# Convolution inputs of a hybrid decoder mixer: transposed by VectorE and transfers in place of TensorE

## The chip, the cores and the metric

The kernel runs on one core of one Trainium2 chip. The metric is the device time of one execution in microseconds; lower is better. Times below are the median of three runs and one profiled execution of the kernel before.

## What is computed

Two layers, each `h += 1/2 norm(SwiGLU(norm(h)))`, then `h += norm(mixer(norm(h)))`, then a second half SwiGLU, on 256 tokens of width 1024 (feed-forward width 2816), all in float32. The mixer projects its input into the columns of three branches; the change concerns the state-space branch (and the feed-forward parts):

```python
q, k, v, z, xbc, dt_raw, u, vg, gate_raw = jnp.split(xn @ w_in, split_at, axis=-1)
xbc = jax.nn.silu(causal_depthwise_conv(xbc, conv_w, conv_b))   # 1536 channels, 4 taps along the tokens
xs, bm, cm = jnp.split(xbc, [SSM_WIDTH, SSM_WIDTH + SSM_GROUPS * SSM_STATE], axis=-1)
dt = jax.nn.softplus(dt_raw.astype(F32) + dt_bias.astype(F32))
y_s = ssd_scan(xs, dt, a, bm, cm) + d_skip[:, None] * xs
```

## The kernel before

**Weights.** All weight matrices are one list of 496 blocks of 128 x 1024 float32. `load` (L160, on SP's queue) brings a block into one of 6 `raw` buffers; `split` makes of it a high part `whi` on ScalarE (L180) and a low part `wlo` on VectorE (L181), in one of 11 pairs of buffers; a matrix product on TensorE takes three matmuls (L213 to L215), high by high, low by high, high by low. Tokens are two tiles of 128.

**The order.** It is written out by the program itself. `gemm` emits the work of TensorE in units of one block and one token tile, six matmuls of 512 columns. After each unit `pump` counts 1.3 us of planned time, steps the tasks that are due (`tick`), and emits the split of one more block if there is one to do. A task is a generator; what it yields is the planned time until its next step, from the table `W`. `finish` steps tasks without regard to what is due, until they have ended. What is emitted first stands first on each engine, and each engine works in that order and waits where data or buffers are not there. A chunk of a projection (512 columns) is eight units.

**Start of a mixer.** `project("xbc", nch=2)` computes the first two chunks of xbc and spawns a task `conv` for each; then come the chunk xbc2 with the third `conv`, z0, z1, the time step (`dt_task`), q0, q1, k and v. In `conv` ScalarE scales the chunk into `xtok` (two tiles, tokens on partitions, L504), TensorE transposes 128 x 128 pieces of it into PSUM (`transposed`, L513), and ScalarE copies them into `xc` (channels on partitions, L516). Then ScalarE writes the last tap and the bias (L535), VectorE adds three taps (L541, twelve instructions a convolution), ScalarE applies silu (L544), and TensorE transposes the result: of convolutions 0 and 1 into `xstr`, which ScalarE copies to `xs` (tokens on partitions again, L553), and the part B of convolution 2 into `btr`. `dt_task` computes `dtps` on TensorE, a chain of small VectorE operations between two exponentials of ScalarE (`dte` L588, `ea` L606), and with the sums `acsT` and `acs` (L620 to L628) what `ssd` starts from. PSUM has five banks for products (`acc`) and three for all else (`tr`). Ahead of `dt_task` the kernel calls `finish(*cv)`, ahead of `ssd` `finish(dte, *ze)`.

**Feed-forward part.** For each of its six chunks `evac` makes `hh`, which `swap_out` transposes in 32 x 32 squares on VectorE into `xt` (L277) and writes to DRAM in one transfer a tile (L279); `swap_in` reads it back in four transfers a tile into `hr` (L286), so that the whole is transposed; then it is split into `hTh` and `hTl` for the down projection (`dn`).

Of the kernel before, what the change touches and what calls it, by code (L numbers as in the profile page):

```python
# [44 lines left out]
ACC, TR = 5, 3  # L45


W = {'gw': 6.5, 'tr': 0, 'parts': 0, 'sq': 1.3, 'lead': 3.9, 'sq2': 5.2, 'hh': 5.2, 'x0': 0.65, 'cv': 5.2, 'cs': 6.5, 'xs': 0, 'dt1': 2.6, 'dt2': 0, 'dt3': 5.2, 'cb': 2.6, 'w1': 1.3, 'w2': 5.2, 'ys': 3.9, 'qk': 3.9, 'vv': 0, 'qs': 0, 'ex': 0, 'p1': 10.4, 'p2': 0, 'p3': 3.9, 'ge': 0, 'ln': 10.4, 'sv': 0, 'yc': 9.1, 'mg': 3.9, 'out': 6.5, 'in': 6.5}


@with_exitstack
def trunk(ctx, tc, a):
# [11 lines left out]
    def b4(name, shape=(P, 1024), dt=F32):  # L64
        return big.tile(list(shape), dt, name=name, tag="b4", bufs=B4)

    def b2(name, shape=(P, 512), dt=F32):
        return big.tile(list(shape), dt, name=name, tag="b2", bufs=B2)
# [203 lines left out]

    def swap_out(src, w):
        xt = b2("xt")
        V.transpose(xt[:, :w], src[:, :w])  # L277
        rd = dram.tile([P, w], F32, name=f"swap{w}", tag=f"swap{w}", bufs=8)
        nc.sync.dma_start(rd, xt[:, :w])  # L279
        return rd  # L280

    def swap_in(dst, rd):

        v = rd.rearrange("(a i) (c e) -> c i a e", a=4, c=4)
        for c in range(4):
            nc.sync.dma_start(dst[32 * c:32 * c + 32], v[c])  # L286

    def halves(ps, hi, lo):

# [105 lines left out]
    def ffn(x, r2, nxt, head=HOLD):  # L395
        hT = {}
        es = {}

        def evac(c, w, gate, up):
            silu, hh = {}, {}  # L400
            for t in range(NT):
                while gate(t) is None:
                    yield 0
                silu[t] = b2("silu")
                A.activation(silu[t][:, :w], gate(t), AF.Silu, scale=r2[t])  # L405
            for t in range(NT):
                while up(t) is None:
                    yield 0
                hh[t] = b2("hh")
                V.scalar_tensor_tensor(hh[t][:, :w], up(t), r2[t], silu[t][:, :w], op0=ALU.mult, op1=ALU.mult)  # L410
            n = w // P
            rd = {t: swap_out(hh[t], w) for t in range(NT)}
            yield W["out"]
            hr = {}
            for t in range(NT):
                hr[t] = b2("hr")
                swap_in(hr[t][:, :w].rearrange("p (a e) -> p a e", a=4), rd[t])
            yield W["in"]
            new = b4 if n > 2 else b2
            hT[c] = (new("hTh", (P, NT, n, P), F32R), new("hTl", (P, NT, n, P), F32R))  # L420
            for t in range(NT):
                hi, lo = (z[:, t].rearrange("p k (a j) -> p a k j", a=4) for z in hT[c])
                r4 = hr[t][:, :w].rearrange("p (a k j) -> p a k j", a=4, k=n)
                A.copy(hi, r4)
                V.tensor_tensor(lo, r4, hi.bitcast(F32), op=ALU.subtract)
                yield 0.65

        def gated(c, w):
            slots, dst = accs("gu")
            full = set()  # L430

            def part(key, o):
                return lambda t: slots[key, t][:, o:o + w] if (key, t) in full else None

            halves_ = 2 if w == 512 else 1
            items = [b for key in range(halves_) for b in chunk(key)]
            es[c] = spawn(evac(c, w, part(0, 0), part(1, 0) if halves_ == 2 else part(0, w)))
            gemm(items, x.h, x.l, dst, head=head if c == 0 else 0, on_done=lambda key, t: full.add((key, t)))

        for c, w in enumerate(FCH):  # L440
            gated(c, w)
        items = [[(k, 512 * j, 512, j, k == 0, k == KF - 1) for j in range(2)] for k in range(KF)]

        def hx(i):
            def get(k, t):
                finish(es[k // 4])
                return hT[k // 4][i][:, t, k % 4, :]
            return get

        slots, dst = accs("dn")  # L450
        after = After(slots, nxt)
        gemm(items, hx(0), hx(1), dst, tail=HOLD, on_done=after, ends=nxt[-1] is not None)
        return after.tasks
# [24 lines left out]
    def mixer(l, x, r2, nxt):  # L478
# [20 lines left out]
        def tokens(ps, scales, name):  # L499

            out = []
            for t in range(NT):
                o = b2(name)
                A.activation(o, ps[t], AF.Copy, scale=scales[t])  # L504
                out.append(o)
            return out
# [18 lines left out]

        def conv(c, ps):
            toks = tokens(ps, r2, "xtok")
            xc = b4("xc", (P, 4, S))
            yield W["x0"]
            yield from transposed(toks, lambda t: xc[:, :, t * P:(t + 1) * P], "a")  # L530
            o = b4("conv", (P, 4, S))
            w = lambda j, k: pl[:, G_CW + 4 * (4 * c + j) + k:G_CW + 4 * (4 * c + j) + k + 1]
            for j in range(4):
                ct = 4 * c + j
                A.activation(o[:, j, :], xc[:, j, :], AF.Identity, scale=w(j, 3),  # L535
                             bias=pl[:, G_CB + ct:G_CB + ct + 1])
            for jj in (0, 2):
                for k in range(3):
                    s = 3 - k
                    for j in (jj, jj + 1):  # L540
                        V.scalar_tensor_tensor(o[:, j, s:], xc[:, j, :S - s], w(j, k), o[:, j, s:],  # L541
                                               op0=ALU.mult, op1=ALU.add)
                yield W["cv"]
            A.activation(o, o, AF.Silu)  # L544
            yield W["cs"]
            if c < 2:
                for t in range(NT):
                    if t not in xs:
                        xs[t] = b4(f"xs{t}")
                    pt = tr("xstr")  # L550
                    for j in range(4):
                        T.transpose(pt[:, j * P:(j + 1) * P], o[:, j, t * P:(t + 1) * P], ident)
                    A.copy(xs[t][:, 512 * c:512 * c + 512], pt)  # L553
                    yield W["xs"]
            else:
                bc["T"] = o
                pt = tr("btr")
                for g in range(SG):
                    T.transpose(pt[:, g * P:(g + 1) * P], o[:, g, 0:P], ident)
                bc["b"] = b2("btok", (P, SG * P))  # L560
                A.copy(bc["b"], pt[:, :SG * P])
# [345 lines left out]
        factors()  # L907
        cv.append(spawn(conv(2, project("xbc")[0])))
        ze = [spawn(z_evac(c, project("z")[0])) for c in range(2)]
        finish(*cv)  # L910
        dte = spawn(dt_task(wdt[l]))
        at = [spawn(qk_evac("q", 0, project("q")[0]))]
        finish(dte, *ze)
        ss = spawn(ssd(ysx, rs))
        at.append(spawn(qk_evac("q", 1, project("q")[0])))
        for c in range(2):
# [218 lines left out]
```

## Time and profile before

| | |
|---|---|
| median of 3 runs | 1486.92 us (1486.62 to 1488.68) |
| profiled execution | 1487.98 us |
| its span, first to last instruction | 1486.2 us |
| TensorE busy | 1472.1 us, 99% |
| VectorE busy | 955.2 us, 64% |
| ScalarE busy | 782.6 us, 53% |
| DMA, share of 16 engines on SP's queue | 60.6%, 291.84 MB |
| chain of waits | TensorE 94%, VectorE 4%, ScalarE 1%, issue 1% |

The span is the time between the first and the last instruction; the execution has 1.78 us more around it. Busy time is the time in which an engine had an instruction at work; of TensorE it contains overlap, since a matmul of 390 ns follows the one before after 227 ns. The chain of waits goes back from the last instruction, at each step to what released it.

### The profile page before, as it was taken

Reading aid. Unit: us, or ns where it says so; the run is one execution under the profiler, and the core shown is the slowest. Engines: PE = TensorE matmul, PEld = TensorE weight load, DVE = VectorE, ACT = ScalarE, POOL = GpSimd, SP = SyncE. Lnnn points to the kernel's source line nnn. Section 1 sums busy time; section 2 is a strip of 40 time slices with the busy share of each in tenths; the row PEclk is TensorE's granted clock in tenths of the full one; section 3 lists DMA queues with packets and bytes.
Section 4 is the critical chain, followed back from the end, with each engine's and each line's share of the span. In section 5 each row is a group of like instructions: output and inputs, shape, how many; then the busy total and the mean of one; then the engine's idle time right before and its main releaser. Section 6 shows DMA issues by size and latency. Waiting matters only on the chain.

```text
span 1486.2 us, 18786 instructions
## 1 busy us (share of the span) xinstructions
PE 1472.1 (99%) x6850; PEld 1218.8 (82%) x6850; DVE 955.2 (64%) x1160; ACT 782.6 (53%) x1079; POOL 55.6 (4%) x98
## 2 busy tenths in 40 slices
PE   9999999999999999999999999999999999999998
PEld 7888888878888888888888888888788888888886
DVE  6766477766666857656486564876665667676652
ACT  6644367555374536544364543765554645464441
POOL 0000020000000000000000000200000000000000
PEclk9999999999999999999999999999999999999999
DMA  8987655335556445888568784654354564478860
GB/s 291 323 253 236 199 190 179 127 115 184 159 181 217 168 154 198 283 230 259 163 230 256 235 253 132 224 167 135 119 192 141 194 204 170 134 272 261 238 200 29
DMA packets 112476, 293.37 MB, mean 197 GB/s; under 512 B 16896, under 2 KB 41600, under 8 KB 112384
## 3 DMA queue, kind: packets, MB, share of 16 engines
q1 hardware_dynamic: 111808, 291.84, 60.6%
q8 instruction: 54, 0.88, 0.2%
q10 hardware_dynamic: 576, 0.33, 0.1%
q14 instruction: 38, 0.31, 0.1%
HBM read 279.54 MB, written 12.58 MB: 197 GB/s over the span
## 4 chain that ended last, share of the span: by engine, by line
PE 94%; DVE 4%; ACT 1%; issue 1%; POOL 0%; DMA 0%; DVEq 0%; ACTq 0%; POOLq 0%
PE gu L213 11%; PE gu L215 11%; PE gu L214 11%; PE dn L213 5%; PE dn L215 5%; PE dn L214 5%; PE br L213 3%; PE br L215 3%; PE br L214 3%; PE gate L215 2%; PE gate L213 2%; PE gate L214 2%; DVE wlo L181 2%; PE xbc L215 1%; PE xbc L213 1%; PE xbc L214 1%
## 5 line engine op out<-in xcount | busy, mean ns | idle before, releaser
L181 DVE TENSOR_TENSOR wlo<-raw,whi 128x1024 fp32r<-128x1024 f32 x495 | 600.2, 1232 | 331.1 <-ACT whi L180 319.8
L180 ACT CAST whi<-raw 128x1024 fp32r<-128x1024 f32 x495 | 512.8, 1051 | 380.9 <-PE gu L215 131.8
L213 PE MATMUL gu<-whi,xh 128*128 128x512 f32 x704 | 276.0, 392 | 1.4 <-ACT xh L316 1.4
L214 PE MATMUL gu<-wlo,xh 128*128 128x512 f32 x704 | 274.9, 391 | 0.0
L215 PE MATMUL gu<-whi,xl 128*128 128x512 f32 x704 | 274.8, 390 | 0.0
L213 PEld LDWEIGHTS gu<-whi,xh 128*128 128x128 f32 x704 | 132.7, 188 | 29.8 <-ACT xh L316 1.8
L215 PEld LDWEIGHTS gu<-whi,xl 128*128 128x128 f32 x704 | 132.6, 188 | 28.0 <-DVE xl L317 0.4
L214 PEld LDWEIGHTS gu<-wlo,xh 128*128 128x128 f32 x704 | 132.5, 188 | 27.9 <-DVE wlo L169 0.9
L213 PE MATMUL dn<-whi,hTh 128*128 128x512 f32 x352 | 137.5, 391 | 0.0
L215 PE MATMUL dn<-whi,hTl 128*128 128x512 f32 x352 | 137.0, 389 | 0.0
L214 PE MATMUL dn<-wlo,hTh 128*128 128x512 f32 x352 | 136.9, 389 | 0.0
L215 PEld LDWEIGHTS dn<-whi,hTl 128*128 128x128 f32 x352 | 66.1, 188 | 13.8
L213 PE MATMUL gate<-whi,xh 128*128 128x512 f32 x192 | 77.3, 403 | 0.0
L214 PEld LDWEIGHTS dn<-wlo,hTh 128*128 128x128 f32 x352 | 66.1, 188 | 13.5
L213 PEld LDWEIGHTS dn<-whi,hTh 128*128 128x128 f32 x352 | 66.1, 188 | 13.4
L215 PE MATMUL gate<-whi,xl 128*128 128x512 f32 x192 | 75.0, 391 | 0.0
L214 PE MATMUL gate<-wlo,xh 128*128 128x512 f32 x192 | 74.8, 390 | 0.0
L316 ACT CAST xh<-xg 128x512 fp32r<-128x512 f32 (+1 forms) x25 | 15.1, 603 | 62.3 <-DVE xg L314 62.3
L215 PEld LDWEIGHTS gate<-whi,xl 128*128 128x128 f32 x192 | 36.0, 188 | 7.7
L405 ACT ACTIVATE silu<-gu,r 128x512 f32<-128x512 f32 (+1 forms) x48 | 31.3, 654 | 19.8 <-PE gu L215 16.2
L214 PEld LDWEIGHTS gate<-wlo,xh 128*128 128x128 f32 x192 | 36.2, 188 | 6.6
L213 PEld LDWEIGHTS gate<-whi,xh 128*128 128x128 f32 x192 | 36.1, 188 | 6.6
(243 smaller groups left out, 2248.3 us busy)
## 6 DMA issues: line engine op xcount, KB each, us to landing
raw<-in_mix SPq DMA_DIRECT2D x232, 512.0 KB, 4.2
raw<-in_gu SPq DMA_DIRECT2D x175, 512.0 KB, 4.9
raw<-in_dn SPq DMA_DIRECT2D x88, 512.0 KB, 4.5
swap<-xt SPq DMA_DIRECT2D x40, 256.0 KB, 3.2
hr<-swap SPq DMA_DIRECT2D x160, 64.0 KB, 4.9
row_ffn_post_g<-in_ffn_post_g SPq DMA_DIRECT2D x4, 512.0 KB, 7.0
swap<-xt SPq DMA_DIRECT2D x8, 128.0 KB, 4.4
hr<-swap SPq DMA_DIRECT2D x32, 32.0 KB, 6.1
```

What stands on the lines that cost most here:

```text
L180: A.copy(hi, w)
L181: V.tensor_tensor(lo, w, hi.bitcast(F32), op=ALU.subtract)
L213: T.matmul(o, xh(k, t), hi[:, off:off + n], start=first, stop=False)
L214: T.matmul(o, xh(k, t), lo[:, off:off + n], start=False, stop=False)
L215: T.matmul(o, xl(k, t), hi[:, off:off + n], start=False, stop=last)
L316: A.copy(o_h, xg)
L405: A.activation(silu[t][:, :w], gate(t), AF.Silu, scale=r2[t])
```

## The change

The feed-forward part transposes `hh` in its own buffer and writes it in four transfers a tile (`turn`), and one transfer a tile reads it back into the same buffer (`land`). The convolution's input no longer goes through TensorE: VectorE transposes `xtok` in place in 32 x 32 squares, four transfers a tile write it to DRAM in pieces of 32 numbers (128 bytes), 512 pieces a transfer (`turn_whole`), and one transfer a convolution reads it into `xc` (`land_whole`). The read can only be issued after the writes have landed. Between the steps stand new yields (2.6, `out`, `in`), and in `W` `out` goes from 6.5 to 7.8 and `in` from 6.5 to 9.1. `finish(*cv)` moves from ahead of `dt_task` to behind q0.

```diff
-W = {... 'out': 6.5, 'in': 6.5}
+W = {... 'out': 7.8, 'in': 9.1}
...
-    def swap_out(src, w):
-        xt = b2("xt")
-        V.transpose(xt[:, :w], src[:, :w])
-        rd = dram.tile([P, w], F32, name=f"swap{w}", tag=f"swap{w}", bufs=8)
-        nc.sync.dma_start(rd, xt[:, :w])
+    def turn(src, m, e=128):
+        V.transpose(src, src)
+        rd = dram.tile([m, 4, 32, 4, e], F32, name=f"turn{m}_{e}", tag=f"turn{m}_{e}", bufs=8)
+        for b in range(4):
+            nc.sync.dma_start(rd[:, :, :, b, :].rearrange("m c i e -> i (m c) e"),
+                              src[32 * b:32 * b + 32].rearrange("p (x e) -> p x e", e=e))
         return rd
...
+    def land(dst, rd):
+        nc.sync.dma_start(dst, rd.rearrange("m c i a e -> (c i) m (a e)"))
+
+    def turn_whole(toks):
+
+        rd = dram.tile([4, P, S], F32, name="turnw", tag="turnw", bufs=6)
+        v = rd.rearrange("k (c i) (t a j) -> t a i (k c) j", c=4, a=4, t=NT)
+        for t in range(NT):
+            V.transpose(toks[t], toks[t])
+            for b in range(4):
+                nc.sync.dma_start(v[t, b], toks[t][32 * b:32 * b + 32, :].rearrange("p (b j) -> p b j", j=32))
+        return rd
+
+    def land_whole(o, rd):
+        nc.sync.dma_start(o, rd.rearrange("k p e -> p k e"))
...
             n = w // P
-            rd = {t: swap_out(hh[t], w) for t in range(NT)}
+            rd = {t: turn(hh[t][:, :w], 1, w // 4) for t in range(NT)}
             yield W["out"]
-            hr = {}
-            for t in range(NT):
-                hr[t] = b2("hr")
-                swap_in(hr[t][:, :w].rearrange("p (a e) -> p a e", a=4), rd[t])
+            for t in range(NT):
+                land(hh[t][:, None, :w], rd[t])
             yield W["in"]
...
         def conv(c, ps):
             toks = tokens(ps, r2, "xtok")
+            yield 2.6
+            rd = turn_whole(toks)
+            yield W["out"]
             xc = b4("xc", (P, 4, S))
-            yield W["x0"]
-            yield from transposed(toks, lambda t: xc[:, :, t * P:(t + 1) * P], "a")
+            land_whole(xc, rd)
+            yield W["in"]
...
         ze = [spawn(z_evac(c, project("z")[0])) for c in range(2)]
-        finish(*cv)
         dte = spawn(dt_task(wdt[l]))
         at = [spawn(qk_evac("q", 0, project("q")[0]))]
-        finish(dte, *ze)
+        finish(dte, *ze, *cv)
```

The changed kernel's lines are twelve higher from L300 on. The transfers of the first mixer's convolutions on SP's queue are new; between weight blocks (`raw`) stand the writes (`turnw`) of convolutions 0 and 1, their reads (`xc`), and the same of convolution 2:

```order
L160 DMA raw<-in_mix 128x1024 x26
L294 DMA turnw<-xtok 32x16x32 x16
L160 DMA raw<-in_mix 128x1024 x3
L298 DMA xc<-turnw 128x4x256 x2
L160 DMA raw<-in_mix 128x1024
L294 DMA turnw<-xtok 32x16x32 x8
L160 DMA raw<-in_mix 128x1024 x3
L298 DMA xc<-turnw 128x4x256
```

Before, only `raw` stands there; now 24 writes and three reads stand between, each read behind the writes it needs.

On TensorE at the end of the chunk q0 of the first mixer, before (the six matmuls of q are the first unit of q1, `cb` the first of `ssd`):

```order
L620 MATMUL acsT<-con,dtg 40x128 x4
L627 MATMUL acs<-dta,con 128x32
L628 MATMUL acs<-dta,ones 128x16
L213 MATMUL q<-whi,xh_1619 128x512
L214 MATMUL q<-wlo,xh_1619 128x512
L215 MATMUL q<-whi,xl_1620 128x512
```

And now:

```order
L633 MATMUL acsT<-con,dtg 40x128 x4
L640 MATMUL acs<-dta,con 128x32
L641 MATMUL acs<-dta,ones 128x16
L565 MATMUL xstr<-con,conv 128x128 x16
L572 MATMUL btr<-con,conv 128x128 x2
L213 MATMUL q<-whi,xh_1595 128x512
```

The eighteen transposes of the convolutions' results, which stood in three places among z0 and z1, stand in one piece between `acs` and q1.

On ScalarE at the same place, from the copy of `dtps` to `dec`, before:

```order
L572 COPY dtT<-dtps 32x256
L180 CAST whi<-raw 128x1024
L588 ACT_TABLE_LOAD
L588 ACTIVATE dte<-dtav 128x32
L606 ACTIVATE ea<-hpar 128x16
L180 CAST whi<-raw 128x1024 x3
L624 CAST acsr<-acsT 40x512
L632 ACTIVATE eac<-acs 128x16
L635 ACTIVATE dec<-dec 128x16
```

And now, from the same copy, and (second piece) from `dec` on:

```order
L585 COPY dtT<-dtps 32x256
L548 ACTIVATE conv<-xc,par 128x256 x4
L180 CAST whi<-raw 128x1024
L601 ACT_TABLE_LOAD
L601 ACTIVATE dte<-dtav 128x32
L557 ACT_TABLE_LOAD
L557 ACTIVATE conv<-conv 128x1024 x2
L619 ACT_TABLE_LOAD
L619 ACTIVATE ea<-hpar 128x16
L180 CAST whi<-raw 128x1024 x3
L637 CAST acsr<-acsT 40x512
L645 ACTIVATE eac<-acs 128x16
```

```order
L648 ACTIVATE dec<-dec 128x16
L566 COPY xs_2376<-xstr 128x512
L566 COPY xs_2383<-xstr 128x512
L566 COPY xs_2376<-xstr 128x512
L566 COPY xs_2383<-xstr 128x512
L557 ACT_TABLE_LOAD
L557 ACTIVATE conv<-conv 128x1024
L574 COPY btok<-btr 128x256
```

The silus (L557) stand between the exponentials and behind `dec`, each with a table load of its own; the copies of `xstr` have moved behind `dec`. On VectorE the same piece now has, between `dtg` and `acsr`, two splits, the last six taps of convolution 2 and a split, where three splits stood; ahead of `dtav` stand the 24 taps of convolutions 0 and 1, the first six of convolution 2 and five splits from the first tap on, in the order 12 taps, three splits, 12 taps, a split, 6 taps, a split.

## Rows read from the trace of the kernel before

**Rows 1.** page, part 1: busy us, share and instructions of each engine

```profile
PE 1472.1 (99%) x6850; PEld 1218.8 (82%) x6850; DVE 955.2 (64%) x1160; ACT 782.6 (53%) x1079; POOL 55.6 (4%) x98
```

**Rows 2.** chain of waits: start us, us, what; transposes of two convolution inputs

```profile
218.52 0.87 PE ctr L513 x8
```

**Rows 3.** timeline of ScalarE, first mixer: start us, us, instruction, [idle before]

```profile
222.22 4.08 ACT L535 ACTIVATE conv<-xc,par 128x256 f32<-128x256 f32 x8
...
237.04 2.00 ACT L544 ACTIVATE conv<-conv 128x1024 f32<-128x1024 f32 x2
...
246.23 1.07 ACT L553 COPY xs<-xstr 128x512 f32<-128x512 f32 x2 [2.10 <-PE xstr L552]
...
259.08 1.28 ACT L588 ACT_TABLE_LOAD   x1
260.94 0.23 ACT L588 ACTIVATE dte<-dtav 128x32 f32<-128x32 f32 x1 [0.58 <-DVE dtav L586]
261.08 0.20 ACT L606 ACTIVATE ea<-hpar 128x16 f32<-128x16 f32 x1
...
270.66 0.22 ACT L635 ACTIVATE dec<-dec 128x16 f32<-128x16 f32 x1 [0.24 <-DVE dec L634]
```

**Rows 4.** timeline of VectorE over the same stretch

```profile
221.44 1.23 DVE L181 TENSOR_TENSOR wlo<-raw,whi 128x1024 fp32r<-128x1024 f32 x1 [0.70 <-ACT whi L180]
222.91 4.91 DVE L541 SCALAR_TENSOR_TENSOR conv<-xc,par,conv 128x253 f32<-128x253 f32 x12 [0.25 <-ACT conv L535]
227.74 3.50 DVE L181 TENSOR_TENSOR wlo<-raw,whi 128x1024 fp32r<-128x1024 f32 x3
231.14 4.82 DVE L541 SCALAR_TENSOR_TENSOR conv<-xc,par,conv 128x253 f32<-128x253 f32 x12
...
260.31 0.37 DVE L582 SCALAR_TENSOR_TENSOR dtv<-dtps,r,hpar 128x16 f32<-128x16 f32 x2
...
264.67 0.20 DVE L609 SCALAR_TENSOR_TENSOR dta<-dt,ea 128x32 f32<-128x32 f32 x1
264.97 0.29 DVE L616 COPY dtg<-dta 128x32 f32<-128x32 f32 x2
...
269.29 0.68 DVE L625 TENSOR_TENSOR acsr<-acsT,acsr 8x512 fp32r<-8x512 f32 x1
```

**Rows 5.** timeline of TensorE, from the end of q0 to q1

```profile
266.85 1.07 PE L620 MATMUL acsT<-con,dtg 128*40 128x128 f32 x8
...
268.32 0.48 PE L213 MATMUL q<-whi,xh 128*128 128x512 f32 x1
```

**Rows 6.** groups by line, VectorE: count | busy us, mean ns | idle before

```profile
L277 DVE STREAM_TRANSPOSE xt<-hh 128x512 f32<-128x512 f32 (+1 forms) x48 | 29.0, 642 | 0.0
```

**Rows 7.** windows (last: clock, DMA share, GB/s); DMA packets from 699.5 to 700.5

```profile
214.00:218.00 4.00, 4.00 (x19) 3.21 (x18) 3.10 (x3) 3.73 (x6) 0.00 (x0) 1.00 1.02 417
...
226.00:230.00 4.00, 4.00 (x19) 3.30 (x18) 4.00 (x7) 3.68 (x5) 0.00 (x0) 1.00 0.05 10
...
DMA packets 338, 0.08 MB, mean 84 GB/s; under 512 B 336, under 2 KB 336, under 8 KB 338
...
q1 hardware_dynamic: 338, 0.08, 37.1%
```

**Rows 8.** transfers of L286, the feed-forward part's reads

```profile
DMA to landing us min/median/max: 1.7/4.9/8.1
```

**Rows 9.** timeline of TensorE and windows after a wait of the first mixer

```profile
310.79 0.63 PE L513 MATMUL ctr<-con,qtok 128*128 128x128 f32 x4 [1.58 <-DVE ssw L682]
...
312.00:314.00 2.00, 2.00 (x6) 1.56 (x5) 1.95 (x3) 1.44 (x3) 0.00 (x0) 0.50 0.00 0
314.00:316.00 2.00, 2.00 (x7) 1.59 (x6) 1.62 (x2) 0.34 (x2) 0.00 (x0) 0.65 0.03 2
```

**Rows 10.** tiles hr and dn, first feed-forward part: ns, first and last start

```profile
L425 DVE TENSOR_TENSOR hTl<-hr,hTh x4: 418/556/686, 137.4 to 151.3; 128x512 fp32r<-128x512 f32 x2, 128x256 fp32r<-128x256 f32 x2
...
L213 PE MATMUL dn<-whi,hTh x88: 389/389/481, 132.2 to 192.2; 128*128 128x512 f32 x88
```

More of the change, by code (lines that the diff above doesn't have):

```diff
@@ L45 @@
 ACC, TR = 5, 3
-W = {'gw': 6.5, 'tr': 0, 'parts': 0, 'sq': 1.3, 'lead': 3.9, 'sq2': 5.2, 'hh': 5.2, 'x0': 0.65, 'cv': 5.2, 'cs': 6.5, 'xs': 0, 'dt1': 2.6, 'dt2': 0, 'dt3': 5.2, 'cb': 2.6, 'w1': 1.3, 'w2': 5.2, 'ys': 3.9, 'qk': 3.9, 'vv': 0, 'qs': 0, 'ex': 0, 'p1': 10.4, 'p2': 0, 'p3': 3.9, 'ge': 0, 'ln': 10.4, 'sv': 0, 'yc': 9.1, 'mg': 3.9, 'out': 6.5, 'in': 6.5}
+W = {'gw': 6.5, 'tr': 0, 'parts': 0, 'sq': 1.3, 'lead': 3.9, 'sq2': 5.2, 'hh': 5.2, 'x0': 0.65, 'cv': 5.2, 'cs': 6.5, 'xs': 0, 'dt1': 2.6, 'dt2': 0, 'dt3': 5.2, 'cb': 2.6, 'w1': 1.3, 'w2': 5.2, 'ys': 3.9, 'qk': 3.9, 'vv': 0, 'qs': 0, 'ex': 0, 'p1': 10.4, 'p2': 0, 'p3': 3.9, 'ge': 0, 'ln': 10.4, 'sv': 0, 'yc': 9.1, 'mg': 3.9, 'out': 7.8, 'in': 9.1}
 @with_exitstack
@@ L271, in sumsq @@
         return ss
-    def swap_out(src, w):
-        xt = b2("xt")
-        V.transpose(xt[:, :w], src[:, :w])
-        rd = dram.tile([P, w], F32, name=f"swap{w}", tag=f"swap{w}", bufs=8)
-        nc.sync.dma_start(rd, xt[:, :w])
-        return rd
[L282 to L286, printed above, removed]
+    def turn(src, m, e=128):
[4 more added lines that the diff above has]
+                              src[32 * b:32 * b + 32].rearrange("p (x e) -> p x e", e=e))
+        return rd
+    def land(dst, rd):
[10 more added lines that the diff above has]
+        nc.sync.dma_start(o, rd.rearrange("k p e -> p k e"))
     def halves(ps, hi, lo):
@@ L422, in evac @@
                 hi, lo = (z[:, t].rearrange("p k (a j) -> p a k j", a=4) for z in hT[c])
-                r4 = hr[t][:, :w].rearrange("p (a k j) -> p a k j", a=4, k=n)
+                r4 = hh[t][:, :w].rearrange("p (a k j) -> p a k j", a=4, k=n)
                 A.copy(hi, r4)
```

## Prediction

> **What bounds the kernel now.** I read the page first: TensorE is busy 1472.1 of 1486.2 us [rows 1], and the chain of waits is 94% TensorE. So an instruction taken off TensorE shortens the kernel by its own time, and an instruction that TensorE has to wait for lengthens it by the wait, at once; ScalarE and VectorE count only where TensorE's next instruction needs their result. Next I read the chain for the transposes that go [rows 2], then the timelines of ScalarE and VectorE over the first mixer's start [rows 3, 4] and the two TensorE rows at the end of its first q chunk [rows 5]. The reader is to see there that in the kernel before the three convolutions are so far by 246.23 that their first outputs are copied [rows 3], long before that point, and that the last step into the q1 chunk, at 268.32, is not waited for. The timeline of the second mixer has the same pieces with the same durations, so I work out one layer and double it.
>
> **What is removed.** Each layer has four groups of input transposes: two of eight instructions at 0.87 us [rows 2] and two of four, at half of it. That is 2.62 us a layer, 5.2 us in all, from the path. ScalarE loses six copies a layer and VectorE gains six in-place transposes of 0.64 us [rows 6]; both lie beside TensorE's work.
>
> **What is added: the trip of the inputs.** The order on VectorE puts the four transposes of convolutions 0 and 1 behind the same split that ended at 222.7 [rows 4]; at 0.64 us each they run to about 225.3, the first write being issued about two transposes in. The DMA engines were full until then (share 1.02 at 214 to 218) and free after 226 (0.05) [rows 7], so the writes flow from about 225. Sixteen transfers of 512 packets of 128 bytes are 8192 packets. No packet of 128 bytes is in the trace. The nearest row is the stretch with 336 packets of 256 bytes: share 37.1% of 16 engines for 1 us over 338 packets, 17.6 ns each [rows 7]. With that price, 8192 x 17.6 / 16 = 9.0 us, done at 234.0. Lower bound half of it (4.5 us, price by bytes), upper bound double (18 us, because these are writes of pieces half as long as any in the row); I take the row itself. Three weight blocks stand between on SP, 0.524 MB each at 417 GB/s [rows 7], 3.8 us, then the read back of the first 0.5 MB, 1.3 us, and at least 1.7 us to land [rows 8]: the first convolution's input is there at **241** (236.5 with the lower bound, 250 with the upper). In the kernel before its first activation began at 222.22 [rows 3]. SP waits for the writes there, with weight loads queued behind it; ten split blocks stand ahead of TensorE, 27 us of its work, so that wait alone starves nobody before about 264.
>
> The Trainium skill, page "DMA: Bandwidth & Descriptors", section "Specifications", says that below 512 bytes a DMA engine does a read-modify-write; no row here shows a write so short. By it I would take the upper bound, 250, and the sum below would be 18 us larger.
>
> **What is moved: the convolutions into the end of q0.** Planned steps are in units of one weight block and one token tile (six matmuls). The yields of a convolution now end beyond the chunk at which it is asked for: the order shows the sixteen output transposes and the two of B forced out in one piece behind acsT, ahead of q1. From the arrival X of the input the engines, which work in order, need:
> - VectorE: first tap 0.7 us behind the first activation; 12 taps 4.9, three weight splits 3.5, 12 taps 4.8, a split 1.2, six taps of convolution 2 at half of twelve, 2.5, a split 1.2, and 0.6 for dtv (0.37) and dtav (0.2, as dta) [rows 4]: X+19.4.
> - ScalarE: dte 0.2, a table load 1.3, the two silus 2.0, a table load back 1.3, ea 0.2 [rows 3]: X+24.4. The loads are new here, because silu now stands between two exponentials; eight more in the program.
> - VectorE: dta and dtg, 0.6 [rows 4]: X+25.0. Only now can acsT start. With the input at 241 that is 266.0; TensorE would be there at 266.85 (its start before [rows 5]) less 2.62 and less the eighteen transposes that used to lie ahead (18 x 0.109 = 2.0, same form as [rows 2]), 262.2. A first wait of 3.8 us.
> - VectorE after it, in order: two splits with a short wait for their other half 2.8, the last six taps 2.5, a split 1.2: X+31.5; then acsr to ScalarE's dec 1.6 [rows 3, 4]: X+33.1. Two of the four transpose groups wait here, since only three PSUM buffers serve them.
> - ScalarE: four xs copies 2.1, a table load 1.3, silu of convolution 2 1.1 [rows 3], then the transposes of B 0.3: **X+37.9**, when q1 can start.
>
> With X = 241 q1 starts at 278.9, against 268.32 before [rows 5]: 10.6 us later a layer, the removed 2.62 us being inside (the wait is 13.2 us). Two layers: 21.2 us. A wait of that length also costs clock: before, after a wait of 1.58 us that ended at 310.79, the granted clock stood at 0.50, the 1.2 GHz level, for the 2 us from 312 and averaged 0.65 over the next 2, some 3.4 us at that level [rows 9], 1.7 us lost. I add 1.7 us a layer, 3.4 (none and 3.4 a layer are the bounds). **Sum: 21.2 + 3.4 = 24.6 us.**
>
> The Trainium skill, page "ScalarE: Activation LUTs", section "What ACT_TABLE_LOAD costs", puts 1.38 us of drain on top of each load; in the trace the load that began at 259.08 and took 1.28 has dte behind it at 260.94, and that waited 0.58 us for VectorE's dtav, for nothing else [rows 3]; I leave the drain out. By the page three loads a layer on the path would add 8.3 us to the sum.
>
> **Feed-forward part: nothing.** It has as many transfers a chunk as before (eight out and two in, for two and eight), as many transposes, and no row of TensorE waits for hT. The new distances put the last chunk 3.9 us later. Its split ended near 152 where the down projection began at 132.2 [rows 10], and that projection has sixteen blocks (16 x 2.7 = 43 us) ahead of the chunk: 20 us of cover. If it were gone, 3.9 us for each of four feed-forward parts.
>
> **The rivals.** (a) The forecast, +24.6 us: 1511.5. (b) The short writes cost double: X = 250, q1 19.6 us later a layer, 39.2 + 3.4 = +42.6 us: 1529.5. For it: nothing in the trace shows that SBUF can be written out in such pieces at the price of longer reads. Against it: the engines are free at that time. (c) On the other side, the trip and the chain are hidden: if X + 37.9 comes ahead of 265.7 (268.32 less 2.62), q1 waits for nothing and the gain is the 5.2 us: 1481.7. That decides at X = 227.8, and breaks even at 230.4. Against it: the transposes alone end at 225.3. For it: parts of my chain might overlap more than the order lets me see. (d) Half hidden, with a wait of some 2.6 us a layer that eats the gain: no change. (e) TensorE runs out of split weights too, because VectorE holds its splits behind taps that wait for data: needs X beyond 257, and gives over 1535.
>
> **How the numbers follow.** The profiled execution took 1487.98 us, 1.78 more than its span; the median of the runs is 1486.92, 1.06 below it. I add the sum to the median: 1486.92 + 24.6 = **1511.5**. Chances: (a) 0.60, (b) 0.22, (c) 0.07, (d) 0.05, (e) 0.06. Range: at the lower bound of the packets X = 236.5, q1 6.1 us later a layer, and no clock lost: +12.2, 1499; I begin the range at 1500. Its upper end is (b) with somewhat more clock lost, 1531. Left out are (c), (d) and (e), 0.18. What a measurement of this kernel can tell from no change is 0.2%, 3 us: faster 0.07, within it 0.05, slower 0.88.
>
> **What would show it.** In the profile after: TensorE idle 11 to 22 us in each mixer between the end of q0 and the start of q1, put down to ScalarE or VectorE at acsT, xstr and btr; a stretch at clock 0.50 there; 14 table loads for 6; the first conv activation some 20 us behind xtok; SP waiting for turnw. Wrong: the first conv activation within 12 us of xtok (then (c)); q1 later than 282 (then (b)); waits of TensorE in the feed-forward parts; or a wait at q0's end without the clock falling.

## The result, and the profile after

The changed kernel takes 1513.68 us, median of 4 runs (1513.32 to 1515.19), beside 1487.63 us for the kernel before on the same chip: ratio 1.0177, 95% interval [1.0165, 1.019]. The forecast was 1511.5, the range 1500 to 1531. The profiled execution took 1513.51 us with a span of 1511.7.

Part 1 of the page after, to be held against [rows 1]:

```profile
PE 1476.1 (98%) x6802; PEld 1221.0 (81%) x6802; DVE 958.4 (63%) x1172; ACT 787.4 (52%) x1075; POOL 57.7 (4%) x98
```

Span less busy time of TensorE was 14.1 us before (1486.2 - 1472.1) and is 35.6 now (1511.7 - 1476.1): 21.5 us more waiting. Busy time rose by 4.0 us although 5.2 us of transposes are gone, because some matmuls run at the lower clock. The view of waits over the whole span, TensorE after (line, released by whom: us in all, times, longest), has three entries that the kernel before does not have:

```profile
PE acsT L633 <- DVE dtg L629: 8.9, 2, 4.8
PE btr L572 <- ACT conv L557: 6.1, 2, 3.0
PE xstr L565 <- DVE acsr L638: 6.1, 2, 3.0
```

21.1 us together, each once in each mixer. There is no new wait in the feed-forward parts. (In `conv` and behind it the lines are thirteen higher, not twelve: L620 before is L633 now.) The timeline of TensorE at the place of [rows 5], first mixer:

```profile
266.43 1.90 PE L633 MATMUL acsT<-con,dtg 128*40 128x128 f32 x8 [4.07 <-DVE dtg L629]
...
273.26 2.82 PE L565 MATMUL xstr<-con,conv 128*128 128x128 f32 x12 [3.04 <-DVE acsr L638]
279.13 0.69 PE L572 MATMUL btr<-con,conv 128*128 128x128 f32 x2 [3.04 <-ACT conv L557]
279.47 0.78 PE L213 MATMUL q<-whi,xh 128*128 128x512 f32 x1
```

The second q chunk, "q1", starts at 279.47 instead of 268.32 [rows 5]. The timeline of ScalarE, to be held against [rows 3]:

```profile
238.85 1.26 ACT L658 ACTIVATE zs<-z,r 128x512 f32<-128x512 f32 x2
241.66 4.05 ACT L548 ACTIVATE conv<-xc,par 128x256 f32<-128x256 f32 x8 [1.55 <-DMA xc<-turnw]
...
260.61 0.23 ACT L601 ACTIVATE dte<-dtav 128x32 f32<-128x32 f32 x1 [2.27 <-DVE dtav L599]
260.86 1.28 ACT L557 ACT_TABLE_LOAD   x1
262.15 2.00 ACT L557 ACTIVATE conv<-conv 128x1024 f32<-128x1024 f32 x2
264.16 1.28 ACT L619 ACT_TABLE_LOAD   x1
265.45 0.21 ACT L619 ACTIVATE ea<-hpar 128x16 f32<-128x16 f32 x1
...
273.89 0.21 ACT L648 ACTIVATE dec<-dec 128x16 f32<-128x16 f32 x1 [0.24 <-DVE dec L647]
...
276.73 1.28 ACT L557 ACT_TABLE_LOAD   x1
278.02 1.06 ACT L557 ACTIVATE conv<-conv 128x1024 f32<-128x1024 f32 x1
```

The first convolution begins at 241.66, before at 222.22 [rows 3]; the silu of two convolutions now stands between dte and ea, with a table load on either side. A line that the next section turns on: ScalarE had z's silu until 240.1 and then waited only 1.55 us for the trip. VectorE, to be held against [rows 4]:

```profile
260.38 0.19 DVE L599 SCALAR_TENSOR_TENSOR dtav<-dtv 128x32 f32<-128x32 f32 x1
...
265.70 0.19 DVE L622 SCALAR_TENSOR_TENSOR dta<-dt,ea 128x32 f32<-128x32 f32 x1 [1.46 <-ACT ea L619]
266.00 0.28 DVE L629 COPY dtg<-dta 128x32 f32<-128x32 f32 x2
...
272.52 0.68 DVE L638 TENSOR_TENSOR acsr<-acsT,acsr 8x512 fp32r<-8x512 f32 x1
```

SP's queue in the timeline, and the landing times of the reads (line L298) from 215 to 262:

```profile
222.72 10.63 SPq L294 DMA_DIRECT2D turnw<-xtok  x16
233.45 1.41 SPq L160 DMA_DIRECT2D raw<-in_mix  x3
234.95 1.26 SPq L298 DMA_DIRECT2D xc<-turnw  x2
```

```profile
DMA to landing us min/median/max: 6.3/6.7/7.6
```

The windows show the clock (third number from the end) falling in the first wait (0.75 from 264 to 266), at the lower level (0.50, 1.2 GHz) up to the start of q1 and back 2.5 us behind it:

```profile
266.00:268.00 2.00, 1.57 (x8) 1.33 (x8) 1.65 (x4) 2.00 (x3) 0.00 (x0) 0.50 0.00 0
...
280.00:282.00 2.00, 2.00 (x6) 1.57 (x5) 0.00 (x0) 1.39 (x3) 0.00 (x0) 0.50 0.00 0
282.00:284.00 2.00, 2.00 (x14) 1.77 (x14) 0.00 (x0) 0.59 (x1) 0.00 (x0) 0.98 0.00 0
```

So the prediction read the chain from the input on to within 0.7 us. But its chain starts at "X, the arrival of the input", and 1.55 us is all that ScalarE waited for it. Whether the trip or something else sets X is what most of the runs are about.

### The profile page after: what moved, and what is told of

Its sections match the earlier page's. It is cut to its first block, busy times and chain, and to the rows that moved or that the text cites. A ratio compares the mean times of both kernels' runs of the same rounds, so it can differ in the third digit from the quotient of the medians.

```text
span 1511.7 us, 18626 instructions
## 1 busy us (share of the span) xinstructions
PE 1476.1 (98%) x6802; PEld 1221.0 (81%) x6802; DVE 958.4 (63%) x1172; ACT 787.4 (52%) x1075; POOL 57.7 (4%) x98
## 4 chain that ended last, share of the span: by engine, by line
PE 88%; DVE 6%; ACT 2%; issue 1%; DMA 1%; POOL 0%; SPq 0%; DVEq 0%; ACTq 0%; POOLq 0%
PE gu L215 10%; PE gu L214 10%; PE gu L213 10%; PE dn L214 5%; PE dn L215 5%; PE dn L213 5%; DVE wlo L181 3%; PE br L215 3%; PE br L214 3%; PE br L213 3%; PE gate L215 2%; PE gate L213 2%; PE gate L214 2%; DVE conv L554 2%; PE xbc L213 1%; PE xbc L214 1%
## 5 line engine op out<-in xcount | busy, mean ns | idle before, releaser
L215 PE MATMUL gu<-whi,xl 128*128 128x512 f32 x704 | 274.8, 390 | 0.0
```

The source lines that it names most:

```text
L215: T.matmul(o, xl(k, t), hi[:, off:off + n], start=False, stop=last)
```

## The experiments

All times are medians; "+" is the distance from the kernel before on the same chip (1486.3 to 1486.9 us; for the changed kernel 1487.6). The input's way begins with `xtok`, and ScalarE starts to write `xtok` (L514) between 215.8 and 217.8 us in these runs. So where the inputs of two runs are compared, the time from there to the first convolution is given too; it is 25.33 us in the changed kernel (241.66 - 216.33).

**Which part of the change?** Three runs. *ffn_only* puts back the old convolution input and the old place of completion:

```
             toks = tokens(ps, r2, "xtok")
-            yield 2.6
-            rd = turn_whole(toks)
-            yield W["out"]
             xc = b4("xc", (P, 4, S))
-            land_whole(xc, rd)
-            yield W["in"]
+            yield W["x0"]
+            yield from transposed(toks, lambda t: xc[:, :, t * P:(t + 1) * P], "a")
...
+        finish(*cv)
         dte = spawn(dt_task(wdt[l]))
         at = [spawn(qk_evac("q", 0, project("q")[0]))]
-        finish(dte, *ze, *cv)
+        finish(dte, *ze)
```

> Only the feed-forward half of the change (the transposes in place on VectorE, 512-byte pieces, the later landing, yields 7.8 and 9.1); the convolutions and the place where they are completed stay as before. The theory (the loss is wholly in the projection stretch): same as before, 1487.6 plus or minus 2. Rival, the halves share the loss because the four longer writes of a chunk hold up weight blocks on the SP queue: a wait of TensorE in the down projections (L213 to L215 on dn, none in before) and 1490 or more.

Measured: 1486.78, ratio 1.0000 [0.9992, 1.0009]. No wait at dn. *finish_only* is the kernel before with one edit:

```
-        finish(*cv)
         dte = spawn(dt_task(wdt[l]))
         at = [spawn(qk_evac("q", 0, project("q")[0]))]
-        finish(dte, *ze)
+        finish(dte, *ze, *cv)
```

> The kernel before with one edit: the convolutions are completed a projection chunk later (behind the first q chunk, with the step-size task and z) and the rest stays. The theory (the place of the completion costs nothing by itself, the late input does): 1487.6 plus or minus 2, first matmul of the second q chunk near 268.3 as in before. Rival, the completion itself, four more tasks forced at one point with their table loads, is the loss: a wait of 3 us or more a layer ahead of the second q chunk, 1494 or more.

Measured: 1487.25, ratio 1.0000 [0.9992, 1.0009]. ScalarE's timeline in this run shows the reason: two convolutions are at their silu by 237.53, so being asked for later costs nothing.

```profile
237.53 2.00 ACT L544 ACTIVATE conv<-conv 128x1024 f32<-128x1024 f32 x2
```

*conv_only* keeps the convolution half and the late completion, and puts the feed-forward part back (`swap_out`, `swap_in`, 6.5 and 6.5).

> Only the convolution half of the change with the later completion; the feed-forward halves swap as before (yields 6.5 and 6.5). The theory: all of the loss, 1513.7 plus or minus 2, second q chunk first at 279.5. Rival, the halves share it: 1500 to 1510.

Measured: 1514.98, 1.0188 [1.0174, 1.0202]. All of the loss is in the convolutions' new input: its trip through DRAM, or the pauses written around it.

**Trip or pauses?** `conv` now yields 2.6 us of matmul time before the writes, 7.8 before the read and 9.1 after it, 19.5 in place of 0.65. These pauses decide where the convolution's instructions stand in the order of ScalarE and VectorE, whether data is late or not. *no_write* keeps the pauses and leaves the writes out:

```
-                nc.sync.dma_start(v[t, b], toks[t][32 * b:32 * b + 32, :].rearrange(...))
+                pass
-        nc.sync.dma_start(o, rd.rearrange("k p e -> p k e"))
+        nc.sync.dma_start(o, <256-wide rows of the first weight block>)
```

> The changed kernel without the convolutions' writes: the transposes and the reads stay, but a read takes four rows of the first weight block instead of the written scratch tensor and waits for no write, so the convolutions work on wrong data. If the order of ScalarE and VectorE is the loss and the trip itself only 1.55 us beyond it: first convolution at 240.1 (right behind z's silu) instead of 241.7, TensorE's waits ahead of the second q chunk shorter by 1.5 to 2.2 a layer, 1509 to 1511. Rival, the short writes are the loss: 1482 to 1492.

Measured: 1510.28, 1.016 [1.0143, 1.0177], +23.9. ScalarE in this run:

```profile
239.03 1.26 ACT L659 ACTIVATE zs<-z,r 128x512 f32<-128x512 f32 x2
240.18 4.04 ACT L549 ACTIVATE conv<-xc,par 128x256 f32<-128x256 f32 x8
...
263.97 0.22 ACT L620 ACTIVATE ea<-hpar 128x16 f32<-128x16 f32 x1
```

Nothing is written, nothing is waited for, and the convolution still starts at 240.18, right behind z's silu; from there ea follows after 23.79 us, exactly as in the changed kernel (265.45 - 241.66 = 23.79). *pauses_only* goes the other way: TensorE transposes as before, but with the pauses.

```
+            xc = b4("xc", (P, 4, S))
             yield 2.6
-            rd = turn_whole(toks)
+            yield from transposed(toks, lambda t: xc[:, :, t * P:(t + 1) * P], "a")
             yield W["out"]
-            xc = b4("xc", (P, 4, S))
-            land_whole(xc, rd)
             yield W["in"]
```

> The changed kernel with the convolutions' inputs transposed by TensorE as before, but with the change's pauses (2.6, 7.8 and 9.1 us of matmul time) kept between, and with the late completion: the new order without the trip. If the order is the loss: the first convolution behind z's silu near 241 to 243, TensorE's waits before the second q chunk 7 to 11 us a layer, 1508 to 1516 (TensorE's 2.6 us of transposes a layer are back). Rival, the trip is the loss: 1486 to 1492.

Measured: 1512.66, 1.0175 [1.0158, 1.0192], +26.0. There is no trip at all in this kernel, and it is as slow as the changed one. Its order is not quite the changed kernel's (a weight split stands between z's silu and the convolution, and TensorE has its 5.2 us of transposes back), so it shows that the order alone can cost this much, not that the two kernels lose the same 26 us at the same places. Its waits of TensorE, and ScalarE's first convolution:

```profile
PE btr L571 <- ACT conv L556: 10.6, 2, 5.5
PE xstr L564 <- DVE acsr L637: 3.9, 2, 2.0
PE acsT L632 <- DVE dtg L628: 3.7, 2, 1.9
```

```profile
241.39 1.26 ACT L657 ACTIVATE zs<-z,r 128x512 f32<-128x512 f32 x2
...
244.11 4.05 ACT L547 ACTIVATE conv<-xc,par 128x256 f32<-128x256 f32 x8
```

**With shorter pauses.** *short* keeps the trip and cuts the pauses:

```
             rd = turn_whole(toks)
-            yield W["out"]
+            yield 5.2
             xc = b4("xc", (P, 4, S))
             land_whole(xc, rd)
-            yield W["in"]
+            yield 5.2
```

> The changed kernel with the two pauses of the convolution's trip cut to 5.2 and 5.2 us of matmul time (from 7.8 and 9.1), so that the convolutions stand earlier in ScalarE's and VectorE's order and two of the three silu stand ahead of the step-size task; the trip itself is the same. If the order of ScalarE and VectorE behind the pauses makes most of the 12 us a layer (the trip alone only 1.55 of them): ScalarE waits for xc by up to 8 us near 230 to 240, with the weight splits behind it covered by the eleven blocks ahead, the chain to acsT begins 2 to 5 us earlier and its table loads fall, 1490 to 1506. Rival, the trip's landing is the loss: the landing moves little, TensorE takes the same wait, 1511 to 1516; if the splits queued behind it run dry, over 1516.

Measured: 1502.13, 1.0114 [1.0096, 1.0132], +15.2: 11 us of the loss are gone, with the same writes and reads. By the clock the data comes hardly sooner (241.19 for 241.66; counted from `xtok` 2.0 us sooner, 23.36, with two weight loads instead of three between the writes and the reads on SP), but what ScalarE does about it has changed:

```profile
241.19 4.05 ACT L548 ACTIVATE conv<-xc,par 128x256 f32<-128x256 f32 x8 [6.19 <-DMA xc<-turnw]
...
254.10 2.08 ACT L548 ACTIVATE conv<-xc,par 128x256 f32<-128x256 f32 x4 [3.93 <-DMA xc<-turnw]
...
261.02 0.34 ACT L585 COPY dtT<-dtps 32x256 f32<-32x256 f32 x1
```

```profile
PE dtps L592 <- ACT dtT L585: 12.8, 2, 7.7
```

Now ScalarE does wait for the trip, 6.19 and 3.93 us, and the copy dtT, which stands behind both on ScalarE, makes TensorE wait at dtps. To see whether that is the whole rest, *short_no_write* has the short pauses and no writes (the two edits above together).

> The short-pause kernel without the convolutions' writes (the read takes rows of a weight block, so the convolutions work on wrong data). If the trip is all of what the short-pause kernel still loses (TensorE's 12.8 us at dtps in both layers, 2.0 at cb): these waits go, TensorE's 5.2 us of transposes are saved, 1482 to 1489. Rival, the order of the short pauses costs by itself: 1494 or more.

Measured: 1484.62, 0.9984 [0.9974, 0.9993], -2.0. The convolution starts at 234.23, the waits at dtps are gone, only 2.0 us at cb stay:

```profile
234.23 4.05 ACT L549 ACTIVATE conv<-xc,par 128x256 f32<-128x256 f32 x8 [0.77 <-DMA xc<-in_gu]
```

The four kernels make a table (us against the kernel before):

| | long pauses (as changed) | short pauses |
|---|---|---|
| writes made | +26.1 | +15.2 |
| writes left out | +23.9 | -2.0 |

The writes cost 2.2 us behind the long pauses and 17.2 behind the short ones; the pauses cost 25.9 without the writes and 10.9 with them. 15.0 us of either are hidden behind the other. The table also says what the change gains with these short pauses when nothing has to be written: 2 us.

**The chain behind X.** *tanh* takes the table loads out of the chain (and replaces silu, so the convolutions' outputs are other numbers):

```
-            A.activation(o, o, AF.Silu)
+            A.activation(o, o, AF.Tanh)
```

> The changed kernel with the convolutions' silu replaced by a tanh, which ScalarE has beside exp, so that the table loads around the step-size task fall from four to one a layer; the outputs of the convolutions are wrong. If these loads stand in the chain to the second q chunk: 2.5 (two loads ahead of ea) to 3.8 us (a third ahead of the last convolution's output) less a layer, 1506 to 1509. Rival, VectorE's taps carry the chain and the loads lie beside them: 1512 to 1515.

Measured: 1508.38, 1.0147 [1.0132, 1.0162], +22.0, so 4.1 us less than the changed kernel. ScalarE in this run:

```profile
242.66 4.05 ACT L548 ACTIVATE conv<-xc,par 128x256 f32<-128x256 f32 x8 [1.81 <-DMA xc<-turnw]
...
263.63 0.20 ACT L619 ACTIVATE ea<-hpar 128x16 f32<-128x16 f32 x1
```

VectorE, and TensorE's wait at btr in the whole span:

```profile
265.34 0.19 DVE L622 SCALAR_TENSOR_TENSOR dta<-dt,ea 128x32 f32<-128x32 f32 x1
```

```profile
PE btr L572 <- ACT conv L557: 3.3, 2, 1.6
```

From the first convolution to ea it is 20.97 us instead of 23.79, 2.8 less, the two loads of 1.28 ahead of ea. But only half of that reaches TensorE: acsT starts 23.41 us behind the first convolution (at 266.07), for 24.77 in the changed kernel. Between dte and dta VectorE has 3.4 us of small operations of its own; here they end last, and dta no longer waits for ea, where it waited 1.46 us in the changed kernel. The load ahead of the last silu counts in full: the wait at btr falls from 3.0 to 1.6 us a layer. To q1 it is 34.59 us from the first convolution instead of 37.81, 3.2 less (the last 0.4 at xstr); the input came 1.0 us later in this run, which takes part of that back. *twice* issues each write twice, the first time into a scratch tensor `turnx` that nobody reads:

```
+        vs = <the same view of the scratch tensor, and of rd>
         for t in range(NT):
             V.transpose(toks[t], toks[t])
-            for b in range(4):
-                nc.sync.dma_start(v[t, b], toks[t][32 * b:32 * b + 32, :].rearrange("p (b j) -> p b j", j=32))
+        for v in vs:
+            for t in range(NT):
+                for b in range(4):
+                    nc.sync.dma_start(v[t, b], toks[t][32 * b:32 * b + 32, :].rearrange("p (b j) -> p b j", j=32))
```

> The changed kernel with every one of the convolutions' writes issued twice, the first time into a scratch tensor that nobody reads. Prediction's rival (b), the writes at double cost: first convolution 9 to 11 us later, near 251, and everything behind it with a slope of one, so 20 to 24 us over the changed kernel, 1533 to 1538 (the working of the prediction said 1529.5). Rival, the chain has slack behind the landing (ScalarE's and VectorE's order carries the loss): under 1522.

Measured: 1540.31, 1.0362 [1.0346, 1.0377], +53.9, more than either theory said.

```profile
246.49 1.05 ACT L180 CAST whi<-raw 128x1024 fp32r<-128x1024 f32 x1 [10.47 <-DMA raw<-in_mix]
...
250.51 4.05 ACT L551 ACTIVATE conv<-xc,par 128x256 f32<-128x256 f32 x8 [1.80 <-DMA xc<-turnw]
...
264.05 1.04 ACT L180 CAST whi<-raw 128x1024 fp32r<-128x1024 f32 x1 [6.66 <-DMA raw<-in_mix]
...
266.14 0.34 ACT L588 COPY dtT<-dtps 32x256 f32<-32x256 f32 x1
```

```profile
PE dtps L595 <- ACT dtT L588: 25.0, 2, 13.0
```

The first convolution is 8.85 us later by the clock and 9.4 counted from `xtok`, as expected. What was not expected is the other way in which the writes work: the weight loads stand behind them on SP, ScalarE's splits wait 10.47 and 6.66 us for those loads, and z's silu and dtT stand behind the splits.

**Could the rest be won back?** Three tries on the short-pause kernel. *lazy_short* forces nothing complete ahead of q1; the state-space task waits in the recording order instead:

```
-        finish(dte, *ze, *cv)
-        ss = spawn(ssd(ysx, rs))
+        def when_ready():
+            while not all(e[2] for e in (dte, *ze, *cv)):
+                yield 0
+            yield from ssd(ysx, rs)
+        ss = spawn(when_ready())
```

> The short-pause kernel where nothing is forced complete behind the first q chunk: the state-space task is spawned as before but its first step waits in the recording order until the step-size, z and convolution tasks are through, so more chunks of projections stand ahead of it on TensorE. In the short-pause run TensorE waits in the first layer for 5.1 us at the step-size matmuls (behind ScalarE's convolution, which waits for its input) and 1.0 us at cb. If only the forced place is at fault in what is left: 1487 to 1490. If ScalarE's wait for the third convolution's input is: the 5.1 stays and 1496 to 1502.

Measured: 1510.59, 1.0166 [1.015, 1.0181], +24.2: neither. The wait at dtps stayed as the second theory said, but the later state-space work met the evacuation of the k chunks on ScalarE:

```profile
PE dtps L592 <- ACT dtT L585: 12.6, 2, 7.0
PE ctr L523 <- ACT qtok L514: 11.1, 4, 4.9
```

*pool_short* issues half of the writes on GpSimd's queue:

```
-                nc.sync.dma_start(v[t, b], ...)
+                (nc.sync if b < 2 else nc.gpsimd).dma_start(v[t, b], ...)
```

> The short-pause kernel with half of the convolutions' writes issued on GpSimd's queue and half on SP's. If the pace at which one queue issues the writes (16 in 9.8 us, 0.61 us each) sets the landing: the first convolution 3 to 5 us earlier, near 237, the wait at dtps of 5.1 and 7.7 us falls to 0 to 3, 1487 to 1496. Rival, the pieces' own time on the DMA engines or GpSimd's slower issue sets it: no earlier, 1500 to 1510.

Measured: 1499.19, 1.0088 [1.0073, 1.0103], +12.5, between the two. The first convolution starts at 239.50, 1.7 us earlier by the clock, but `xtok` is 1.8 us earlier too (216.03 for 217.83): counted from there the input is no sooner in the first layer (23.47 us for 23.36), and 1.4 us sooner in the second (24.25 for 25.60). TensorE's wait at dtps is 9.0 us in both layers for 12.8. *short_wide* keeps 24 writes and their bytes a layer but writes pieces of 2 KB:

```
-                nc.sync.dma_start(v[t, b], toks[t][32 * b:32 * b + 32, :].rearrange("p (b j) -> p b j", j=32))
+                nc.sync.dma_start(<32 rows of 512 numbers in a row>, toks[t][32 * b:32 * b + 32, :])
```

> The short-pause kernel with the same 24 writes a layer and the same bytes, but each row of 512 numbers written in one piece of 2 KB instead of 16 pieces of 128 bytes; the scratch tensor is then not transposed across the 32-blocks, so the convolutions work on wrong data. If the number of pieces is the trip's price: the first convolution at 234 to 237 instead of 241.2, the waits at dtps (12.8 us in both layers) go, 1484 to 1490. Rival, the number of writes, or the path through the scratch tensor (write, then read), is the price: first convolution after 239, 1496 to 1503.

Measured: 1499.70, 1.0086 [1.0069, 1.0103], +13.4, on the rival's side in time, though the convolution came before the rival's 239: at 238.17, 3.0 us earlier by the clock and 1.9 counted from `xtok` (21.45 for 23.36). The wait at dtps is 7.3 us for 12.8. The time of one issue on SP and POOL (ns, min/median/max) in *short*, then in *pool_short*, then in *short_wide*:

```profile
L294 SPq DMA_DIRECT2D turnw<-xtok x16: 325/502/1227, 224.2 to 233.5; - x16
```

```profile
L294 POOL DMA_DIRECT2D turnw<-xtok x12: 648/648/847, 222.7 to 234.8; - x12
L294 SPq DMA_DIRECT2D turnw<-xtok x10: 326/1086/2419, 222.4 to 235.6; - x10
```

```profile
L295 SPq DMA_DIRECT2D turnw<-xtok x19: 302/421/1189, 223.1 to 235.5; - x19
```

With half of the writes on another queue, an issue on SP takes twice as long (1086 for 502), so the two queues share a limit. With a sixteenth of the pieces an issue still takes 421, so the pieces are not the whole price of a write. And the DMA engines were not full when writes alone were moving: their share was 0.76 and 0.79 from 230 to 234 in *short*, 0.55 and 0.57 from 228 to 232 in *short_wide*. The Trainium skill, page "DMA: Bandwidth & Descriptors", section "Rules for kernel authors", says that spreading transfers over issuing engines brings no bandwidth because they share the same 16 engines. The trace agrees that it brought none: from 230 to 234 *pool_short* moved 114 and 111 GB/s, *short* 117 and 122. What holds a write at 0.4 to 0.5 us, its issue on SP, its bytes or something behind both queues, was not separated and stays open. No kernel here that makes the convolutions' writes beats the kernel before; *short_no_write*, 2.0 us faster, leaves them out.

## Why the prediction was right, point by point

- **What is removed, 2.62 us a layer.** Right in size: in *short_no_write* q1 of the first layer starts at 265.70, 2.62 us ahead of 268.32. In the changed kernel it is worth nothing, since TensorE stands waiting at the end of q0 in any case. Even *short_no_write* gained only 2.0 of the 5.2 us; TensorE waits 2.0 us at cb there.
- **The trip, X = 241.** Measured 241.66; its parts were off and cancelled. The writes began at 222.7, not 225, and their issue took 10.6 us, not 9.0, so they ended at 233.4, as forecast to 0.6. The weight loads between took 1.5 us on the queue, not 3.8. The read took 6.3 to 7.6 us from issue to landing, not 3.0: the prediction added a minimum to a bare transfer time where the row had a median of 4.9 for transfers of 64 KB [rows 8], and weight loads of the read's own 0.5 MB landed after a median of 4.2 in the kernel before. The writes ahead of it are not the reason: in *no_write*, where none are made, the reads landed after 5.5 to 6.8. 2.3 too much and some 3.6 too little. In part that is one cost counted in another place, for the bytes of the three weight loads move while the read is under way (DMA share 1.02 and 1.01 from 236 to 240).
- **The price of a piece.** The sum took 17.6 ns on a DMA engine, with all engines at work. The changed kernel's own pieces, in the view of its transfers from 229 to 233 (packets, MB, share), where nothing else moved:

```profile
q1 hardware_dynamic: 3864, 0.48, 78.5%
```

Worked out as in the prediction, 78.5% of 16 engines for 4 us over 3864 packets, that is 13.0 ns a piece, so 6.7 us for the 8192; pieces half as long as in the row cost three quarters of it, and the double price of the upper bound was not there. The writes took 10.6 us all the same, with the engines not full, and *short_wide* still needs 21.45 of 23.36 us with a sixteenth of the pieces. The step "such pieces cost what the row says" came near the right duration with a price too high and a limit that was not the one; that is luck.
- **What sets the start of the chain.** This is the step that failed, without moving the number. The prediction let the convolution start when its input arrives. *no_write* shows that it starts at 240.2 even if it waits for nothing, because the pauses put it behind z's silu on ScalarE. That the trip ended within 1.6 us of this place is luck for the forecast, which has the pauses nowhere in its sum. The order makes rival (c) unreachable by any speed of the trip: its point of decision, X = 227.8, would have needed other pauses. And with other pauses that point is another: *short_no_write* starts at 234.23, later than the 230.4 at which the prediction breaks even, and gained 2.0 us where X + 37.9 would have lost 7.6. And the lower bound of the range was too low: 1500 followed from X = 236.5, while the pauses hold X at 240.2 and the time at about 1510.
- **The chain from X.** dtav ready by X+19.4 = 261.1 with the measured X: 260.57. ea by X+24.4 = 266.1: 265.66. acsT from X+25.0 = 266.7: 266.43. dec done by X+33.1 = 274.8: 274.10. q1 at X+37.9 = 279.6: 279.47. *no_write* shows that it moves as one piece with X: acsT 24.77 and q1 37.81 us behind the first convolution in both kernels. In another order it does not hold (q1 at X+34.60 in *pauses_only*, X+41.78 in *twice*). Of the two loads ahead of ea only some 1.4 us lie in it (*tanh*); the prediction left out VectorE's 3.4 us between dte and dta, which run beside the loads and cover the rest. The Trainium skill, page "ScalarE: Activation LUTs", section "What ACT_TABLE_LOAD costs", adds a drain of 1.38 us to a load; the load at 260.86 took 1.28 and the silu behind it began at 262.15, 0.01 us later; dte had ended at 260.84, 0.02 us ahead of the load. The measurement decides: no drain here.
- **The wait and the clock.** Forecast were a wait of 13.2 us a layer and 1.7 us of lost clock, the latter from a row with a shorter wait. TensorE's waits are 10.2 us in the first mixer and 10.9 in the second, just under the 11 to 22 of the sign. The rest of the stretch is work at the lower clock: from 266.43 to q1, acsT, acs and the eighteen transposes took 7.0 us without the waits, where the prediction's rows make 3.5 of them (1.47 from acsT to q1 [rows 5] and 2.0). Most of that lies beside the chain of ScalarE and VectorE. What counts for the time is q1 behind 279.47, where 2.5 us of matmuls run at 1.2 GHz: some 1.2 us. The first layer's k chunk ends 12.3 us later (11.15 at the start of q1 and 1.2). The second layer loses 13 us, because its first convolution starts 0.9 us later in the layer (747.7 us behind the first layer's, where q1 before lies 734.5 apart and the first layer has lost 12.3); from there to q1 it is 37.73 us, as in the first. Forecast 12.3 a layer.
- **The other signs.** 14 table loads for 6 came, and the first activation 23 us behind xtok. SP hardly waited for the writes: the view of its waits from 210 to 270 has 0.2 us ahead of the reads (L298).
- **Feed-forward part: nothing.** Right (*ffn_only*).
- **Rival (b), the writes at double cost.** *twice* gave its X (250.5 for 250) and missed its time (+53.9 for +42.6). The prediction priced only the convolution's wait; the loads of weights queued on SP behind the writes, and dtT behind the splits on ScalarE, came on top: TensorE waits 12.5 us a layer at dtps, and q1 starts 41.78 us behind X (292.29), not 37.9. It had named that queue and held it harmless until 264 because TensorE's blocks last so long; but it is ScalarE, in its order, that passes the wait on.

## What to carry to other kernels

A pause in a hand-ordered schedule is not free when the data is early, nor is data free when the pause is long: instructions stand where the pause puts them, and everything that stands behind them in an in-order engine moves along. So price a trip twice, by the arrival of its data and by its place in the order of each engine, and take the later of the two; and before building such a trip, run the new order without it (as *pauses_only*) and the trip without its cost (as *no_write* and *short_no_write*): here the first lost 26 us, and the second lost 23.9 with the long pauses (*no_write*) and gained 2 with the short ones, which would have settled the matter. Where two causes hide each other, undoing one alone tells nearly nothing of the other (2.2 or 17.2 us for the same writes).

## What the runs showed of the hardware

- A write of 512 pieces of 128 bytes took SP a median of 502 ns to issue, one of 32 pieces of 2 KB still 421; sixteen of either took 9.8 and 8.3 us, so pieces sixteen times longer bought 1.5 us.
- A written piece of 128 bytes works out at 13.0 ns on a DMA engine in the changed kernel from 229 to 233, with the engines 78.5% busy, where a piece read in the kernel before, twice as long, works out at 17.6 [rows 7].
- When GpSimd issued half of the writes, SP's issue of one went from a median of 502 to 1086 ns, and no more bytes moved (114 and 111 GB/s for 117 and 122).
- A read of 0.5 MB, beside weight loads, landed 6.3 to 7.6 us after its issue behind such writes and 5.5 to 6.8 without them (*no_write*), where the feed-forward part's reads of 64 KB in the kernel before landed after 4.9 [rows 8].
- A table load of 1.28 us is followed by its activation after 0.01 us.
